# A buffer pool of their own for the gates' results, and three DMAs instead of eight for each piece of the SwiGLU weights' sums

## The chip, the cores and the metric

The kernel runs on one core of a Trainium2 chip. A core has TensorE (PE in the profile: matmuls; PEld is its loading of weights), VectorE (DVE), ScalarE (ACT), GpSimd (POOL) and SyncE (SP), which here issues all DMAs. TensorE writes to PSUM, of which this kernel uses eight banks of 128 x 512 float32; everything else lies in SBUF or in HBM. The metric is the device time of one execution in microseconds, smaller is better.

## The reference

The input x has 512 tokens of 1024 channels, all in float32. One decoder block is computed:

```
h = rmsnorm(x, norm1_g);  z = h @ w_in + b_in          # 1024 -> 6656
z_glu, z_rx, z_rg, z_ga, z_gb = split(z)               # 2048, 1280, 1280, 1024, 1024
u  = z_glu[:, :1024] * sigmoid(z_glu[:, 1024:])
u  = silu(layernorm(depthwise_conv31(u)));             y_a = u @ conv_w_out + conv_b_out
xb = depthwise_conv4(z_rx)
r, i = sigmoid(xb @ wa + ba), sigmoid(xb @ wx + bx)    # block-diagonal, 16 blocks of 80
a  = exp(-8 r softplus(-lambda));  b = sqrt(1 - a^2) * (i * xb)
hb = scan over tokens: hb[t] = a[t] hb[t-1] + b[t]
y_b = (hb * gelu(z_rg)) @ lru_w_out
x  = x + (sigmoid(z_ga) * y_a + sigmoid(z_gb) * y_b) @ w_mix_out
h  = rmsnorm(x, norm2_g)
x  = x + (silu(h @ ffn_w1) * (h @ ffn_w3)) @ ffn_w2    # SwiGLU, 2816 wide
out = rmsnorm(x, norm_f_g)
```

## The kernel before

**Number format.** A float32 operand is split into a high part and a low remainder (`split_to`, L115: ScalarE casts the high part, L117; VectorE or POOL subtracts, L113), and each product is three matmuls: high x high, high x low, low x high (`mm3`, L428).

**Weights.** All weight tiles stand in one list, in the order of their use (`wchunk`, L132). `emit_chunk` (L135) loads the next into one of four raw buffers (`raws`), splits it into one of five buffers (`hls`), and `weights` keeps the list four tiles ahead of the matmuls (`AHEAD`).

**First part, channels on partitions.** The list `ORDER` (L201) interleaves the tiles of z, 128 channels by 512 tokens each: `u` (GLU, two tiles of z), `rx` (input of the recurrence, `xb`, its split parts and the pieces `ext` of neighbouring blocks that DMAs copy, L697), `g` (gates), `r` (recurrence), `rg`, `gb` and `ga`. VectorE's 31 taps of the long convolution (`cv`, L596) are run a few at a time beside all of them.

A gate, `gates(j)` (L702), makes two PSUM banks of 4 or 6 matmuls each (L717). ScalarE takes Tanh of the first into the buffer `th` (L722) and of the second in place (L723), then Exp into the buffer `ea` (L726) and another Tanh in place (L727); VectorE follows with L728 to L731, where L731 is the last to read the first bank. `th` and `ea` last until the recurrence of the same number, `recur(j)` (L736), which takes a bank `mu` of its own for the square root (L739), multiplies (L740) and scans (L741). In `ORDER` no more than three gates stand between their `g` and their `r`.

**Buffers.** `tiles(tag, bufs)` (L91) makes a pool of buffers of 128 x 512. `longt` has 65 (`SLOTS`) and holds nearly everything that lasts: the normalized input, `u`, `xb`, `th`, `ea`, the sigmoids, the products and later the operands of the last matmuls. `shortt` has 5. PSUM has six banks for matmuls (`bank`) and two for convolution and the like (`bank2`).

**Later parts.** `yb` (L784) and `ya` (L895) are the two output projections. `w_mix_out`, part of SwiGLU's first weights (k = 2 to 5, `SEVEN`) and `ffn_w2` are multiplied as 2 x 2 blocks in seven products instead of eight, for which four sums t1 to t4 of the weights' blocks are needed. `Sevenfold.pair` (L821) makes the operands of k (`s1p`, `e`, and their parts), `run` (L842) the products. For w_mix_out and ffn_w2 the sums are made by `make_sums` (L276) on VectorE, in raw buffers. For SwiGLU's first weights `make_f_sums` (L314) makes them during the first part: there are 16 pieces; of each, four DMAs load four blocks of 128 x 256 into a buffer of the pool `wsums` (two buffers, L332), POOL makes four sums in place (L337 to L340), and four DMAs store them (L345) into DRAM tiles, one for each sum and k. A DMA of `f_chunk` (L307) reads a whole sum back as a weight tile during SwiGLU.

**Who sets the order.** The kernel is not written as queues. A planner takes the program and lays out each engine's queue before it runs: what is ready by its own estimates goes first, in the order of the code among what is ready. An instruction that writes a new buffer needs a free one of its pool. At run time each engine takes its queue in order, and semaphores hold back an instruction whose operands or buffers are not ready. `issue_after` puts an instruction behind a named one of the same engine; the weight sums' loads and stores stand behind the newest load of a weight tile (`newest["load"]`), and POOL's sums behind its newest subtraction. Some parts (the start, the end of the mix) are laid out by hand.

Of the kernel before, what the change touches and what calls it, by code (L numbers as in the profile page):

```python
# [8 lines left out]
F32 = mybir.dt.float32  # L9
# [4 lines left out]
P = 128  # L14
T = 512
# [13 lines left out]
NF = DF // P  # L29


SLOTS, SHORT = 65, 5
RAW = 4
HL = 5
AHEAD = 4
# [8 lines left out]
SEVEN = (2, 3, 4, 5)  # L44
# [36 lines left out]
def tile_block(ctx, tc, a, out):  # L81
    nc = tc.nc
# [8 lines left out]
    def tiles(tag, bufs):  # L91
        p_ = pool(tag, bufs)
        return lambda name, dtype=F32: p_.tile([P, T], dtype, tag=tag, name=name)

    longt, shortt = tiles("long", SLOTS), tiles("short", SHORT)

    def pairt(name, dtype=F32R):

# [13 lines left out]
    def sub(eng, o, x, y):  # L112
        return eng.tensor_tensor(out=o, in0=x, in1=y, op=ALU.subtract)  # L113
# [18 lines left out]
    def wchunk(key, src, kt, cols, where="hl", lo=pool_e, after=None):  # L132
        chunks.append((key, src, kt, cols, where, lo, after))
# [89 lines left out]
    dram = ctx.enter_context(tc.tile_pool(name="dram", bufs=1, space=bass.MemoryType.DRAM))  # L223
# [68 lines left out]
    w1 = a["ffn_w1"][0].rearrange("(k p) n -> p k n", p=P)  # L292
    w3 = a["ffn_w3"][0].rearrange("(k p) n -> p k n", p=P)


    KF = NF // 2
    f_sums = {(n, k): dram.tile([P, 1024], F32, tag=f"f{n}_{k}", name=f"f{n}_{k}") for k in SEVEN for n in ("t1", "t2", "t3", "t4")}

    def f_quarter(n, k, w_, c0, c1):

        c, j = 4 * (int(n[1]) - 1), k + KF * (int(n[2]) - 1)
        return w_[:, c + c0 : c + c1, j * P : (j + 1) * P]

    def f_chunk(n, k):
        def load(raw_t):
            if n[0] == "t":
                nc.sync.dma_start(raw_t, f_sums[n, k][:, :])  # L307
            else:
                for i, w_ in enumerate((w1, w3)):
                    nc.sync.dma_start(raw_t[:, i * T : (i + 1) * T].rearrange("p (k n) -> p k n", k=4), f_quarter(n, k, w_, 0, 4))  # L310

        wchunk(f"f{n}_{k}", load, 8, P, lo=vec)

    def make_f_sums():  # L314

        todo = [(k, i, c) for k in SEVEN for i in range(2) for c in (0, 2)]
        sums_due, stores_due = [], []
        n = 0  # L320
        while todo or sums_due or stores_due:
            if stores_due and emitted[0] >= stores_due[0][0]:
                stores_due.pop(0)[1]()
            if sums_due and n >= sums_due[0][0]:
                sums_due.pop(0)[1]()
            if todo and n >= SUMS_AT and (n - SUMS_AT) % SUMS_STEP == 0:
                k, i, c = todo.pop(0)
                raw = wsums.tile([P, 1024], F32, tag="wsum", name=f"fws{k}_{i}_{c}")
                q = [raw[:, 256 * m : 256 * m + 256] for m in range(4)]
                with tc.issue_after(newest["load"]):  # L330
                    for m, v in zip(("b11", "b12", "b21", "b22"), q):
                        nc.sync.dma_start(v.rearrange("p (k n) -> p k n", k=2), f_quarter(m, k, (w1, w3)[i], c, c + 2))  # L332

                def sums(q=q, k=k, at=T * i + P * c):
                    q11, q12, q21, q22 = q
                    with tc.issue_after(newest["sub"]):
                        sub(pool_e, q22, q22, q12)  # L337
                        sub(pool_e, q12, q12, q11)
                        pool_e.tensor_tensor(out=q11, in0=q22, in1=q11, op=ALU.add)
                        sub(pool_e, q21, q21, q11)  # L340

                    def stores():
                        with tc.issue_after(newest["load"]):
                            for m, v in (("t1", q12), ("t2", q11), ("t3", q22), ("t4", q21)):
                                nc.sync.dma_start(f_sums[m, k][:, at : at + 256], v)  # L345
# [24 lines left out]
    at, col, parts = 0, {}, []  # L370
    for name, n in ROWS:
# [4 lines left out]
        while done < n:  # L376
            m = min(n - done, P - row_at(at + done)[1])
# [161 lines left out]
    ab, e, s, s2, po, c4 = (sm[:, i, :] for i in range(6))  # L539
# [162 lines left out]
    def gates(j):  # L702
        hv, lv = (gate_view(v[:, 0, :]) for v in weights(f"gate{j}"))
        j5 = j % 5
        banks = []
        for g in range(2):
            ps = bank(f"g{j}_{g}")
            (wh, oh), (wl, ol) = ((v[:, g, 0, :], v[:, g, 1, :]) for v in (hv, lv))
            xh, xl = xbp[j]
            mms = [(wh, xh), (wh, xl), (wl, xh)]  # L710
            if j5 % 2:
                eh, el = ext[j]
                mms += [(l[:MANY], r[:MANY]) for l, r in ((oh, eh), (oh, el), (ol, eh))]
            else:
                mms.append((oh[: 3 * FEW], ext[j][0][: 3 * FEW]))
            for k, (l, r) in enumerate(mms):
                pe.matmul(ps, l, r, start=k == 0, stop=k == len(mms) - 1)  # L717
            banks.append(ps)

        r_, i_ = banks  # L720
        th = longt(f"th{j}")
        act.activation(th, r_, AF.Tanh, scale=0.5, bias=bh[:, 0, j : j + 1])  # L722
        act.activation(i_, i_, AF.Tanh, scale=0.5, bias=bh[:, 1, j : j + 1])  # L723
# [4 lines left out]
        vec.scalar_tensor_tensor(out=r_, in0=A, scalar=1.0, in1=r_, op0=ALU.add, op1=ALU.mult)  # L728
        vec.scalar_tensor_tensor(out=xb[j], in0=i_, scalar=1.0, in1=xb[j], op0=ALU.add, op1=ALU.mult)
        vec.tensor_scalar(out=A, in0=r_, scalar1=1.0, scalar2=None, op0=ALU.add)  # L730
        vec.scalar_tensor_tensor(out=th, in0=A, scalar=1.0, in1=r_, op0=ALU.add, op1=ALU.mult)  # L731
        rec[j] = A, th

    rec = {}

    def recur(j):  # L736
        A, m2 = rec.pop(j)
        mu = bank(f"mu{j}")
# [67 lines left out]
    class Sevenfold:  # L806
# [14 lines left out]
        def pair(self, k, ua, va):  # L821

            n = self.name
            u_ = split(f"{n}us{k}", ua, vec)
            s1 = shortt(f"{n}s1{k}")[:, LO]
            add(s1, va[:, LO], va[:, HI])
            sp = longt(f"{n}s1p{k}", F32R)
            split_to(sp[:, LO], sp[:, HI], s1, vec)
            e = longt(f"{n}e{k}")
            sub(vec, e[:, HI], ua[:, LO], va[:, LO])  # L830
            sub(vec, va[:, LO], s1, ua[:, LO])
            sub(vec, e[:, LO], ua[:, HI], va[:, LO])
            self.ops.append((u_, sp, e, va))
# [58 lines left out]
    for n, j in enumerate(mixq.order()):  # L892
# [3 lines left out]
        o = sga[j]  # L896
# [262 lines left out]
```

## Time and profile before

| | us |
|---|---|
| median of 3 runs (lowest, highest) | 814.06 (813.77, 814.31) |
| the profiled execution | 816.61 |
| its span, first to last instruction | 814.8 |
| TensorE busy | 801.8 (98%) |
| VectorE busy | 648.0 (80%) |
| ScalarE busy | 445.2 (55%) |
| POOL busy | 210.2 (26%) |
| moved by DMA | 153.47 MB, 188 GB/s in the mean |

All rows but the first are of one profiled execution. Its own time is 2.55 above the median of the runs, so a sum of its durations is compared with 816.61. Times in the text count from its first instruction. A row of a timeline gives start, duration, engine, line, operation, what is written and read, and in brackets the idle time of the engine before it and what ended that. A row of waits gives who waited for whom, the total in us, the number and the longest. Rows for the 40 slices of the span give the busy share in tenths; `PEclk` is TensorE's granted clock. Durations of matmuls overlap, since they are pipelined: their cost is the distance from start to start. Names of tiles stand without the buffers' numbers.

### The profile page before, as it was taken

The page shows a single profiled execution, that of the slowest core. Times are in us where ns is not written, and L with a number is a line of the kernel's source. Part 1 is how long each engine was busy: PE and PEld are TensorE (multiplying, and loading weights), DVE is VectorE, ACT ScalarE, POOL GpSimd, SP SyncE. Part 2 cuts the span into 40 slices and gives each one's busy share as a digit, 9 for nine tenths or more (in the row PEclk, how much of TensorE's full clock was granted, in tenths as well). Part 3 has the DMA queues.
Part 4 walks back from the last instruction along what each step waited for, and adds up shares of the span by engine and source line. Part 5 has one row for each costly group of instructions (what it writes and reads, how often), then busy time and mean ns, then how long its engine had stood idle before and what let it go on. Part 6 is the DMA issues. An engine that isn't in the chain of part 4 may idle for free.

```text
span 814.8 us, 11572 instructions
## 1 busy us (share of the span) xinstructions
PE 801.8 (98%) x4038; PEld 683.9 (84%) x4038; DVE 648.0 (80%) x1010; ACT 445.2 (55%) x627; POOL 210.2 (26%) x156
## 2 busy tenths in 40 slices
PE   8999999999999999999999999999999999999996
PEld 7988888887788888888888898999988888888885
DVE  4699899999999987787868869797866665688556
ACT  7546688777668855554336454374632233476443
POOL 3565778758665740000000042000000000000000
PEclk9999999999999999999999999999999999999998
DMA  7746466567565532358737525788778788576552
GB/s 209 192 123 163 131 186 204 169 192 194 163 190 156 167 88 65 101 174 256 234 106 245 156 92 177 243 251 262 227 237 264 251 286 283 185 261 210 173 167 104
DMA packets 183309, 153.47 MB, mean 188 GB/s; under 512 B 13799, under 2 KB 151443, under 8 KB 183251
## 3 DMA queue, kind: packets, MB, share of 16 engines
q1 hardware_dynamic: 183251, 152.73, 61.1%
q8 instruction: 32, 0.52, 0.3%
q14 instruction: 26, 0.21, 0.1%
HBM read 123.46 MB, written 26.21 MB: 184 GB/s over the span
## 4 chain that ended last, share of the span: by engine, by line
PE 92%; DVE 3%; DMA 1%; issue 1%; SPq 1%; POOL 0%; ACT 0%; POOLq 0%
PE z L437 31%; PE f L437 19%; PE or L840 13%; PE fr L1016 10%; PE yb L437 7%; PE ya L437 5%; PE mxr L840 5%; PE g L717 2%; DMA raw_in<-in_w_in_dram 1%; DVE cv L596 1%; SPq L393 1%; PE th L477 0%; DVE xb8l L113 0%; SPq L386 0%; POOL hl_in L113 0%
## 5 line engine op out<-in xcount | busy, mean ns | idle before, releaser
L596 DVE SCALAR_TENSOR_TENSOR cv<-u,par,cv 128x511 f32<-128x511 f32 (+17 forms) x240 | 162.8, 730 | 1.1 <-ACT cv L593 0.9
L113 POOL TENSOR_TENSOR hl_in<-raw_in,hl_in 128x1024 fp32r<-128x1024 f32 x52 | 125.4, 2415 | 92.7 <-ACT hl_in L117 90.2
L117 ACT CAST hl_in<-raw_in 128x1024 fp32r<-128x1024 f32 x52 | 54.2, 1043 | 10.2 <-PE z L437 6.6
L117 ACT CAST hl_f<-raw_f 128x1024 fp32r<-128x1024 f32 x28 | 29.3, 1051 | 51.4 <-DMA raw_f<-in_ffn_w_dram 37.7
L113 DVE TENSOR_TENSOR hl_f<-raw_f,hl_f 128x1024 fp32r<-128x1024 f32 x28 | 36.3, 1308 | 16.4 <-ACT hl_f L117 16.4
L990 POOL TENSOR_TENSOR hf<-h20h,h20l 128x512 f32<-128x512 f32 x1 | 1.3, 1287 | 172.4 <-DVE h20l L481 172.4
L117 ACT CAST hl_ob<-raw_ob 128x1024 fp32r<-128x1024 f32 (+1 forms) x23 | 23.4, 1016 | 38.9 <-PE or L840 18.6
L437 PE MATMUL z<-h10h,hl_in 128*128 128x512 f32 (+1 forms) x112 | 42.9, 385 | 1.5 <-DVE xb L741 1.2
L113 DVE TENSOR_TENSOR hl_ob<-raw_ob,hl_ob 128x1024 fp32r<-128x1024 f32 (+1 forms) x23 | 27.1, 1177 | 20.3 <-ACT hl_ob L117 20.2
L437 PE MATMUL z<-h11h,hl_in 128*128 128x512 f32 (+1 forms) x112 | 42.2, 378 | 0.0
L437 PE MATMUL z<-h12h,hl_in 128*128 128x512 f32 (+1 forms) x112 | 41.9, 376 | 0.0
L437 PE MATMUL z<-h15h,hl_in 128*128 128x512 f32 (+1 forms) x112 | 41.7, 374 | 0.0
L437 PE MATMUL z<-h14h,hl_in 128*128 128x512 f32 (+1 forms) x112 | 41.7, 374 | 0.0
L437 PE MATMUL z<-h13h,hl_in 128*128 128x512 f32 (+1 forms) x112 | 41.7, 374 | 0.0
L437 PE MATMUL z<-h16h,hl_in 128*128 128x512 f32 (+1 forms) x112 | 41.7, 374 | 0.0
L437 PE MATMUL z<-h17h,hl_in 128*128 128x512 f32 (+1 forms) x112 | 41.7, 374 | 0.0
L113 POOL TENSOR_TENSOR fws<-fws 128x256 f32<-128x256 f32 x48 | 36.3, 756 | 2.4
L113 DVE TENSOR_TENSOR ows<-ows,ows 128x512 f32<-128x512 f32 x22 | 15.2, 690 | 19.8 <-DMA ows<-in_ffn_w_dram 19.7
L113 DVE TENSOR_TENSOR hl_ot<-raw_ot,hl_ot 128x1024 fp32r<-128x1024 f32 (+1 forms) x17 | 20.1, 1191 | 11.8 <-ACT hl_ot L117 11.4
L117 ACT CAST hl_ot<-raw_ot 128x1024 fp32r<-128x1024 f32 (+1 forms) x17 | 17.5, 1028 | 17.2 <-PE or L840 15.5
L437 PEld LDWEIGHTS z<-h10h,hl_in 128*128 128x128 f32 x112 | 21.4, 191 | 6.3 <-ACT g L723 1.6
L437 PEld LDWEIGHTS z<-h11h,hl_in 128*128 128x128 f32 x112 | 21.4, 191 | 3.9
(905 smaller groups left out, 2582.3 us busy)
## 6 DMA issues: line engine op xcount, KB each, us to landing
raw_in<-in_w_in_dram SPq DMA_DIRECT2D x52, 512.0 KB
raw_f<-in_ffn_w_dram SPq DMA_DIRECT2D x28, 512.0 KB
ows<-in_ffn_w_dram SPq DMA_DIRECT2D x22, 512.0 KB
ot<-ows SPq DMA_DIRECT2D x44, 256.0 KB
raw_ob<-in_ffn_w_dram SPq DMA_DIRECT2D x33, 256.0 KB
raw_ot<-ot SPq DMA_DIRECT2D x33, 256.0 KB
fws<-in_ffn_w_dram SPq DMA_DIRECT2D x64, 128.0 KB
ft<-fws SPq DMA_DIRECT2D x64, 128.0 KB
```

The source lines that it names most:

```text
L113: return eng.tensor_tensor(out=o, in0=x, in1=y, op=ALU.subtract)
L117: copy(h, full)
L393: nc.sync.dma_start(xt[t][h], x_nat[:, t, h * T : (h + 1) * T])
L437: pe.matmul(ps, l, r, start=i == 0, stop=i == n - 1)
L596: vec.scalar_tensor_tensor(out=acc[c][:, s:], in0=u[c][:, : T - s], scalar=dw(c, s), in1=acc[c][:, s:], op0=ALU.mult, op1=ALU.add)
L717: pe.matmul(ps, l, r, start=k == 0, stop=k == len(mms) - 1)
L840: pe.matmul(banks[i], l_[:, ts], r_, start=start and n == 0, stop=stop and n == 2, skip_group_check=again)
L990: pool_e.tensor_tensor(out=v, in0=h2p[c][0].bitcast(F32), in1=h2p[c][1].bitcast(F32), op=ALU.add)
L1016: pe.matmul(ps[:, HALVES[i]], lw[:, 4 * i + c, :], rx_, start=not (again or i or c or m), stop=bool(i and c == 3 and m == 2), skip_group_c ...
```

## The change

First, the pool of 65 becomes one of 59, and a new pool of six buffers, `gatet`, takes `th` and `ea` of the gates. In the last stage the operands `oe0` to `oe5` of the last product's first six k take buffers of the new pool too. The number of buffers together stays 65.

Second, the four sums of SwiGLU's first weights of one k lie in one DRAM tile of 128 x 4 x 1024 in the order in which they stand in the SBUF buffer (t2, t1, t4, t3). So a piece is stored by one DMA instead of four. It is loaded by two DMAs instead of four, each of them two neighbouring blocks of 128 x 256. The sums themselves, and when they are asked for, are the same. The read back takes the same amount from the new tile, whose rows of 4 KB for one sum lie 16 KB apart.

```diff
-SLOTS, SHORT = 65, 5
+SLOTS, SHORT, GATES = 59, 5, 6
...
-    longt, shortt = tiles("long", SLOTS), tiles("short", SHORT)
+    longt, shortt, gatet = tiles("long", SLOTS), tiles("short", SHORT), tiles("gate", GATES)
...
-    f_sums = {(n, k): dram.tile([P, 1024], F32, tag=f"f{n}_{k}", name=f"f{n}_{k}") for k in SEVEN for n in ("t1", "t2", "t3", "t4")}
+    F_SUMS = ("t2", "t1", "t4", "t3")
+    f_sums = {k: dram.tile([P, 4, 1024], F32, tag=f"fs{k}", name=f"fs{k}") for k in SEVEN}
...
-                nc.sync.dma_start(raw_t, f_sums[n, k][:, :])
+                nc.sync.dma_start(raw_t, f_sums[k][:, F_SUMS.index(n), :])
...
+                four = (w1, w3)[i].rearrange("p (h k) (e n) -> p h k e n", h=2, e=2)
                 with tc.issue_after(newest["load"]):
-                    for m, v in zip(("b11", "b12", "b21", "b22"), q):
-                        nc.sync.dma_start(v.rearrange("p (k n) -> p k n", k=2), f_quarter(m, k, (w1, w3)[i], c, c + 2))
+                    for h in range(2):
+                        nc.sync.dma_start(
+                            raw[:, h * T : h * T + T].rearrange("p (e k n) -> p e k n", e=2, k=2),
+                            four[:, h, c : c + 2, :, k * P : (k + 1) * P].rearrange("p k e n -> p e k n"),
+                        )
...
-                            for m, v in (("t1", q12), ("t2", q11), ("t3", q22), ("t4", q21)):
-                                nc.sync.dma_start(f_sums[m, k][:, at : at + 256], v)
+                            nc.sync.dma_start(f_sums[k][:, :, at : at + 256], raw.rearrange("p (m n) -> p m n", m=4))
...
-        th = longt(f"th{j}")
+        th = gatet(f"th{j}")
...
-        A = longt(f"ea{j}")
+        A = gatet(f"ea{j}")
...
-            e = longt(f"{n}e{k}")
+            e = (gatet if n == "o" and k < GATES else longt)(f"{n}e{k}")
```

More of the change, by code (lines that the diff above doesn't have):

```diff
@@ L329, in make_f_sums, with sums @@
                 q = [raw[:, 256 * m : 256 * m + 256] for m in range(4)]
+                four = (w1, w3)[i].rearrange("p (h k) (e n) -> p h k e n", h=2, e=2)
                 with tc.issue_after(newest["load"]):
-                    for m, v in zip(("b11", "b12", "b21", "b22"), q):
-                        nc.sync.dma_start(v.rearrange("p (k n) -> p k n", k=2), f_quarter(m, k, (w1, w3)[i], c, c + 2))
-                def sums(q=q, k=k, at=T * i + P * c):
+                    for h in range(2):
[3 more added lines that the diff above has]
+                        )
+                def sums(raw=raw, q=q, k=k, at=T * i + P * c):
                     q11, q12, q21, q22 = q
```

## The prediction

> **What bounds the kernel now.** I read, in this order: the page's busy times and slices, the waits of TensorE, TensorE's timeline where those waits lie, then the timelines of ScalarE and VectorE just ahead of them, and last the issues of the weight sums' DMAs on SP.
>
> ```profile
> PE 801.8 (98%) x4038; PEld 683.9 (84%) x4038; DVE 648.0 (80%) x1010; ACT 445.2 (55%) x627; POOL 210.2 (26%) x156
> PE   8999999999999999999999999999999999999996
> DVE  4699899999999987787868869797866665688556
> PEclk9999999999999999999999999999999999999998
> ```
> ```profile
> PE z L437 <- DVE xb L741: 1.2, 1, 1.2
> ...
> PE g L717 <- DVE th L731: 0.6, 1, 0.6
> ```
>
> TensorE is the bound: from 26 to 805 us its slices are full. One 128x512 matmul starts 0.227 us after the one before it (202.56 after 202.33 below). So whatever does not take a gap out of TensorE's row gives nothing, and there are few gaps to take. After the start-up only two waits exceed half a microsecond, both for VectorE, and both lie in one place:
>
> ```profile
> 202.01 0.48 PE L717 MATMUL g<-xb7h,hl_gate 128*128 128x512 f32 x1
> 202.33 0.39 PE L717 MATMUL g<-xb7l,hl_gate 128*128 128x512 f32 x1
> 202.56 0.40 PE L717 MATMUL g<-xb7h,hl_gate 128*128 128x512 f32 x1
> ...
> 203.82 0.50 PE L717 MATMUL g<-xb7h,hl_gate 128*128 128x512 f32 x1 [0.63 <-DVE th L731]
> ...
> 206.24 0.77 PE L437 MATMUL z<-h10h,hl_in 128*128 128x512 f32 x1 [1.22 <-DVE xb L741]
> 206.80 0.63 PE L437 MATMUL z<-h10l,hl_in 128*128 128x512 f32 x1
> ...
> 209.72 0.39 PE L437 MATMUL z<-h12h,hl_in 128*128 128x512 f32 x1
> ```
>
> From 202.01 to 206.24 lie 8 matmuls (8 x 0.227 = 1.82), so 4.23 - 1.82 = 2.41 us were stood. The next 8, from 206.24 to 209.72, took 3.48 us at half the granted clock instead of 1.82: 1.66 more. The place costs 4.07 us. TensorE waits there for PSUM banks: gate 7's second bank was gate 6's first (read last by L731), the next `z` bank was that of recurrence 4 (read last by the scan, L741). Why these were late:
>
> ```profile
> 185.88 0.66 ACT L723 ACTIVATE g<-g,bh 128x512 f32<-128x512 f32 x1 [0.88 <-PE g L717]
> ...
> 189.78 0.62 ACT L117 CAST xb8h<-xb 128x512 fp32r<-128x512 f32 x1 [2.27 <-DVE xb L674]
> ...
> 192.31 0.68 ACT L722 ACTIVATE th<-g,bh 128x512 f32<-128x512 f32 x1
> ```
> ```profile
> 197.44 3.31 DVE L596 SCALAR_TENSOR_TENSOR cv<-u,par,cv 128x501 f32<-128x501 f32 x5
> 200.66 0.68 DVE L728 SCALAR_TENSOR_TENSOR g<-ea,g 128x512 f32<-128x512 f32 x1
> ...
> 203.10 0.67 DVE L731 SCALAR_TENSOR_TENSOR th<-ea,g 128x512 f32<-128x512 f32 x1
> ```
>
> Gate 6 writes two Tanh. The code has `th` (L722) first, and its bank was complete by 184.5. Yet L723 ran at 185.88, ScalarE then sat idle 2.27 us, and `th` came at 192.31, right behind `xb8h`. The difference: L722 writes a new buffer of the pool of 65, L723 writes in place. Laying the code's list of those buffers on their first writes in the trace, I find them in the code's order but for some microseconds throughout: `th6` is asked for behind `xb8`, `xb8h`, `xb8l`, and came behind them. Gates 1, 2 and 4 show the same inversion (second Tanh at 87.7, 109.2, 138.2; first at 91.3, 114.5, 139.7).
>
> **The change part by part.**
>
> *Gates' own pool.* `th6` no longer stands behind the `xb8` buffers. The six gate buffers last belonged to gate 3 and were free at 161.6, so `th6` can run beside the second Tanh at about 186, 6.3 us earlier. The chain behind it (Exp 0.82, Tanh 0.76, L728 to L731 3.1) moves with it, by up to 6.3 us: the bank wanted at 202.9 is then free at about 197, and of the 2.3 us by which recurrence 4's bank was late for 203.8, the three gate operations taken out of VectorE's last stretch give 2.0 (3 x 0.68), and the square roots at 200.4, moved ahead on a freer ScalarE, the rest. Bounds: nothing (the wait stands) to -4.07 (both waits and the half clock go). I take -4.07, since both banks' lateness is the chain's. What is late next: nothing within the next microseconds; margins below.
>
> The half-clock stretch follows the stand: the granted clock is 1.00 up to 206.2, half to 209.6, and 1.00 again. The Trainium skill (TensorE: Matmul & The Clock Gate, "What's actually happening") puts the throttle after an idle window of about 3.4 us; here 2.4 us of stand in two pieces were enough, so trace and page differ. By the page alone, removing the stand would not remove the 1.66 us, and the sum would be -2.41.
>
> The pool's own waits: a gate now waits for the gate three before it. The trace never holds more than six such buffers (144 to 156 and 196 to 206 us), so six suffice; the tightest is `ea7` at 207.03, 0.94 us behind the end of the scan that frees `ea4`. Behind `ea7` on ScalarE stand weight casts, and no weight tile of `z` is split less than 7.2 us before its first matmul: cost 0, with that cover gone at most the lateness of the scan.
>
> *59 buffers for the rest.* Without gates' buffers and `oe0` to `oe5` the trace holds 60 four times: over by one for 0.19 us at 310.8, 0.19 at 316.1, 0.42 at 322.1 and 5.76 at 370.2 to 376.0 (`mxt41l`, until `yb7` frees `y0`). The first three delay a sigmoid or a cast while the PSUM banks near there have over 3 us to spare: 0. The fourth holds one of four raw buffers, so the mix weights' load at 371.07 and, behind it in SP's queue, that of conv_w_out at 375.14 issue up to 5.8 us later; that tile is split 11.0 us before its matmul: 0, and even the whole 5.8 is under 11.0. From 688 to 703 all 65 are held before and 59 + 6 after: no difference. From 720 to 742 the rest holds up to 61: the splits `oeb`, `ovb` wait about one step of k (18 x 0.227 = 4.1 us). Those of k = 7 to 10 are used from 776 on (747.5 + 7 x 4.1): 0, upper bound in the rivals. `oe0` to `oe5` find the gate pool empty since 272.
>
> *Three DMAs a piece.*
>
> ```profile
> L332 SPq DMA_DIRECT2D fws<-in_ffn_w_dram x64: 383/468/697, 34.9 to 255.1; - x64
> L345 SPq DMA_DIRECT2D ft<-fws x64: 383/480/1232, 66.1 to 275.5; - x64
> ```
> ```profile
> SPq L332 <- DMA ft<-fws: 18.5, 16, 3.4
> ```
>
> Before: 64 x 0.468 + 64 x 0.480 = 60.7 us of SP. After: 32 loads of 256 KB in 512 B pieces (nearest row: `raw_fb`, same size and piece, 0.499) = 16.0, and 16 stores of 512 KB (nearest: `raw_in`, 512 KB, 0.385; `ft`, 1 KB pieces, 0.480) = 6.2 to 7.7. SP gains 37 to 39 us. Bytes and pieces stay: 512 B in, 1 KB out, 4 KB back. A load still waits for the store two pieces before (18.5 us in 16 waits, at most 3.4); the store starts as one, up to 3 x 0.48 = 1.4 us of issue sooner, but lands whole, so that wait grows by at most 1.4 x 14 = 20 us, less than is freed. Queued behind are the loads of `z` weights and gates, with the 7.2 us above. TensorE's list has no wait for a weight's DMA, so this gives 0; as bounds I take -0.3 (the wait for hl_in, all that TensorE lists for `z` weights) and +1.4 (one store's issue uncovered once). POOL's 64 operations are the same. The read back has the same 4 KB pieces, only further apart; the nearest tile (`hl_ft4_2`) has 1.7 us to spare: 0.
>
> *Sum.* -4.07 + 0. The profiled execution took 816.61 (span 814.8): 812.5. The median shown, 814.06, is 2.55 below that execution; the same step from it gives 810.0.
>
> **The rivals.**
>
> *The stall stays or moves (814.1).* All engines' queues are laid out anew in advance, and VectorE stays as full (281.1 busy of the 300 us from 30 to 330) on the same six banks. Margins elsewhere are thin: the banks of `z23` (161.1), `z33` (261.5) and `z4` (111.2) were free 0.67, 0.73 and 0.89 us before use. Against: these too hang on gates or recurrences, which come earlier. One like the present gives 814.1; two give 818.1.
>
> *Split waits in the last stage (slower).* Place: 720 to 748, k = 7 to 10, where 59 buffers are up to two short. Price: if ScalarE stands one step (4.1) at a split ahead of a weight cast, a tile with 2.9 (747.5) or 4.05 us (727.1) to spare is up to 1.2 us late; with a half clock, 2.9. Four times: 810.0 + 11.6 = 821.6. It decides from two on (815.8). For: ScalarE already follows TensorE by 0.06 to 2 us there. Against: the casts stand earlier in the code.
>
> *The half clock stays (811.6).* If the slow stretch came by itself, only 2.41 goes: 811.6. Against: it begins at the 206.2 at which TensorE resumes.
>
> **How the numbers follow.** Forecast 0.55, its own range 809.0 to 811.8 (a remaining wait of up to 1.8). Stall stays or moves 0.20; two stalls 0.10; last stage 0.10; half clock 0.05. About 0.2% (1.6 us) is what a measurement of this kernel can tell from no change. Faster (below 812.4): 0.55 + 0.05 less the edges, 0.59; same: 0.20; slower: 0.21. The range 809.0 to 818.5 holds all but most of the last-stage case, the upper half of two stalls and a little below 809.
>
> **What would show it.** Right: in every gate L722 directly beside L723; no wait of TensorE for L731 or L741; granted clock 1.00 from 30 to 800; 32 loads and 16 stores on the sums' lines; SP's wait there under 39 us. Wrong: a new wait of TensorE for VectorE between 60 and 330 with a half-clock slice behind it; one for ScalarE's casts between 720 and 760; or L722 still behind casts of `xb`.

## The result, and the profile after

The changed kernel takes 819.36 us (median; 818.94 to 820.82), the kernel before, beside it, 814.18 (813.32 to 816.03). The ratio is 1.0064 (95% interval 1.0053 to 1.0074): slower by 5.2 us, where 4.1 us less was forecast. The profiled execution took 819.27 (span 817.4) against 816.61. The line numbers of the changed kernel are larger by up to 5: L717 of before is L722 now, L722 and L723 are L727 and L728, L731 is L736.

The engines' totals, from the page of the changed kernel:

```profile
PE 801.2 (98%) x4038; PEld 684.6 (84%) x4038; DVE 646.3 (79%) x1010; ACT 443.0 (54%) x625; POOL 211.2 (26%) x156
```

They say nothing; each is within 3 us of before. The waits of TensorE in the changed kernel do (who waits for whom, total, number, longest):

```profile
PE g L722 <- DMA ext<-xb6h: 4.4, 1, 4.4
...
PE fr L1021 <- ACT c L1033: 0.7, 1, 0.7
```

The two waits of gate 7, for L731 and the scan, are gone, as forecast. A wait at gate 5 has come, not for VectorE but for a DMA: the copies of `xb6`'s rows into `ext5`. TensorE's timeline there:

```profile
159.27 0.39 PE L722 MATMUL g<-xb5h,hl_gate 128*128 128x512 f32 x1
164.02 0.47 PE L722 MATMUL g<-ext,hl_gate 96*128 96x512 f32 x1 [4.36 <-DMA ext<-xb6h]
...
165.28 0.63 PE L722 MATMUL g<-ext,hl_gate 96*128 96x512 f32 x1
...
168.21 0.39 PE L442 MATMUL z<-h12h,hl_in 128*128 128x512 f32 x1
```

From 159.27 to 164.02 are 4.75 us for one step of 0.227: 4.52 stood. The 11 steps from 164.02 to 168.21 took 4.19 instead of 2.50, most of them at half the granted clock: 1.69 more. The place costs 6.2 us. A wait of 0.7 in SwiGLU (L1021, at 543.4) costs 0.8. Against that stand the 4.07 that went at gate 7: +2.9, and the two profiled executions differ by 2.66.

At gate 7 the mechanism of the forecast worked. VectorE's last read of gate 6's first bank:

```profile
198.55 0.68 DVE L736 SCALAR_TENSOR_TENSOR th<-ea,g 128x512 f32<-128x512 f32 x1
```

It starts 4.5 us earlier than the 203.10 of before, though TensorE came to gate 7 5.7 us later (207.7 against 202.0); the bank was free in time for either. ScalarE now takes gate 6's first Tanh at 190.58 and the second at 193.30, in the code's order; in all ten gates the first now comes ahead of the second, where in four of before it came behind.

The DMAs of the weights' sums in the changed kernel (minimum, median and maximum ns, start of first and last), and SP's wait for their stores:

```profile
L335 SPq DMA_DIRECT2D fws<-in_ffn_w_dram x32: 602/643/740, 34.5 to 255.7; - x32
L350 SPq DMA_DIRECT2D fs<-fws x16: 571/596/1768, 66.0 to 275.5; - x16
```
```profile
SPq L335 <- DMA fs<-fws: 41.3, 11, 6.3
```

SP spends 32 x 0.643 + 16 x 0.596 = 30.1 us on issuing instead of 60.7, and waits 41.3 instead of 18.5, once 6.3 us.

Where the lateness of the copies comes from is seen by going back along the queues. Around 140 us the changed kernel has, on ScalarE, GpSimd and SP:

```profile
142.37 0.62 ACT L118 CAST xb5h<-xb 128x512 fp32r<-128x512 f32 x1 [6.31 <-DVE xb L679]
142.89 1.04 ACT L118 CAST hl_in<-raw_in 128x1024 fp32r<-128x1024 f32 x1
...
148.30 0.60 ACT L118 CAST hl_gate<-raw_gate 128x512 fp32r<-128x512 f32 x1
```
```profile
144.01 3.01 POOL L114 TENSOR_TENSOR hl_in<-raw_in,hl_in 128x1024 fp32r<-128x1024 f32 x1 [6.80 <-ACT hl_in L118]
...
154.23 0.52 POOL L184 MEMSET raw_gate<- 128x512 f32 x1
```
```profile
152.56 1.35 SPq L335 DMA_DIRECT2D fws<-in_ffn_w_dram  x2
154.01 0.58 SPq L145 DMA_DIRECT2D raw_in<-in_w_in_dram  x1
154.78 2.85 SPq L189 DMA_DIRECT2D raw_gate<-in_lru_wa_dram  x5
157.68 2.57 SPq L189 DMA_DIRECT2D raw_gate<-in_lru_wx_dram  x4
160.37 0.57 SPq L702 DMA_DIRECT2D ext<-xb6h  x1
```

The same steps in the kernel before:

```profile
136.68 0.62 ACT L117 CAST xb5h<-xb 128x512 fp32r<-128x512 f32 x1
...
139.22 0.62 ACT L117 CAST hl_gate<-raw_gate 128x512 fp32r<-128x512 f32 x1
```
```profile
147.97 0.54 POOL L183 MEMSET raw_gate<- 128x512 f32 x1
```
```profile
154.55 0.54 SPq L697 DMA_DIRECT2D ext<-xb6h  x1
```

`xb5h` is 5.7 us late and the first copy 5.8. `xb5` itself is late on VectorE: its three operations start at 138.9 instead of 133.2, behind 96 taps of the long convolution where it stood behind 90 (a tap takes 0.65 us, so the six are 3.9). The rest comes from two waits of VectorE for ScalarE near 101 us, 0.62 ahead of a `u` and 1.35 ahead of a tap, which the kernel before does not have. The experiments ask which part of the change does this, and which of these links carries it.

### The profile page after: what moved, and what is told of

Same layout as the page of the kernel before. It is cut to its first block, busy times and chain, and to the rows that moved or that the text cites. A ratio compares the mean times of both kernels' runs of the same rounds, so it can differ in the third digit from the quotient of the medians.

```text
span 817.4 us, 11473 instructions
## 1 busy us (share of the span) xinstructions
PE 801.2 (98%) x4038; PEld 684.6 (84%) x4038; DVE 646.3 (79%) x1010; ACT 443.0 (54%) x625; POOL 211.2 (26%) x156
## 2 busy tenths in 40 slices
DMA packets 182029, 153.46 MB, mean 188 GB/s; under 512 B 12519, under 2 KB 150163, under 8 KB 181971
## 4 chain that ended last, share of the span: by engine, by line
PE 80%; DVE 13%; DMA 3%; ACT 2%; POOL 1%; issue 1%; SPq 0%; POOLq 0%; ACTq 0%; DVEq 0%
PE z L442 26%; PE f L442 16%; PE or L845 13%; PE yb L442 7%; PE fr L1021 6%; PE ya L442 5%; DVE cv L601 5%; PE mxr L845 5%; PE g L722 1%; DVE xb L679 1%; PE tx L482 1%; DVE hl_fb L114 1%; DMA raw_ft<-fs 1%; POOL hl_in L114 1%; DMA raw_fb<-in_ffn_w_dram 1%
## 5 line engine op out<-in xcount | busy, mean ns | idle before, releaser
L601 DVE SCALAR_TENSOR_TENSOR cv<-u,par,cv 128x511 f32<-128x511 f32 (+16 forms) x240 | 162.2, 728 | 2.3 <-ACT cv L598 2.2
L442 PE MATMUL z<-h16h,hl_in 128*128 128x512 f32 (+1 forms) x112 | 41.7, 374 | 0.0
L442 PE MATMUL z<-h17h,hl_in 128*128 128x512 f32 (+1 forms) x112 | 41.7, 374 | 0.0
L114 DVE TENSOR_TENSOR ows<-ows,ows 128x512 f32<-128x512 f32 x22 | 15.2, 689 | 20.8 <-DMA ows<-in_ffn_w_dram 20.6
L679 DVE SCALAR_TENSOR_TENSOR xb<-z,par,xb 128x511 f32<-128x511 f32 (+2 forms) x30 | 22.2, 741 | 4.2 <-ACT xb L677 4.0
```

Source lines behind the costliest of these rows:

```text
L442: pe.matmul(ps, l, r, start=i == 0, stop=i == n - 1)
L601: vec.scalar_tensor_tensor(out=acc[c][:, s:], in0=u[c][:, : T - s], scalar=dw(c, s), in1=acc[c][:, s:], op0=ALU.mult, op1=ALU.add)
L679: vec.scalar_tensor_tensor(out=o[:, s:], in0=ps[:, : T - s], scalar=lw(s), in1=o[:, s:], op0=ALU.mult, op1=ALU.add)
```

## The experiments

Every kernel ran beside the kernel before on the same chip; its median was 814.68, 815.17, 814.68 and 814.80 in the four groups. "Stood" is the distance between two neighbouring starts of TensorE less 0.227. The start-up of the profiled executions differs: its last matmul comes between 26.3 and 28.2 us, and all times behind it move with that.

### One part of the change alone

Theory 1: the single store lands late, the next load into its buffer waits, and the copies behind it come late. Rival 1: the gates' pool alone lays the queues out anew, and that makes them late. The gates' pool alone:

```diff
-SLOTS, SHORT = 65, 5
+SLOTS, SHORT, GATES = 59, 5, 6
...
-        th = longt(f"th{j}")
+        th = gatet(f"th{j}")
...
-        A = longt(f"ea{j}")
+        A = gatet(f"ea{j}")
...
-            e = longt(f"{n}e{k}")
+            e = (gatet if n == "o" and k < GATES else longt)(f"{n}e{k}")
```

> The gates' pool (59 + 6 buffers) alone; loads and stores of the sums as before. Theory 1 (the single store lands late, the next load waits for it in SP's queue, and the DMAs of ext behind it come late for gate 5): no single store, so no stand at gate 5, and the stand at gate 7 is gone too: 810 to 812. Rival 1 (the gates' pool lays the queues out so that xb6 and ext come late, whatever the stores do): the stand at gate 5 stays, 817 to 820. Rival 2 (only both together do it): 810 to 812 here and about 814 for the DMAs alone.

The three DMAs alone (pool of 65; the lines that declare the tensors are those of the change), and each half of them:

```diff
...
-                    for m, v in zip(("b11", "b12", "b21", "b22"), q):
-                        nc.sync.dma_start(v.rearrange("p (k n) -> p k n", k=2), f_quarter(m, k, (w1, w3)[i], c, c + 2))
+                    for h in range(2):
+                        nc.sync.dma_start(
+                            raw[:, h * T : h * T + T].rearrange("p (e k n) -> p e k n", e=2, k=2),
+                            four[:, h, c : c + 2, :, k * P : (k + 1) * P].rearrange("p k e n -> p e k n"),
+                        )
...
-                            for m, v in (("t1", q12), ("t2", q11), ("t3", q22), ("t4", q21)):
-                                nc.sync.dma_start(f_sums[m, k][:, at : at + 256], v)
+                            nc.sync.dma_start(f_sums[k][:, :, at : at + 256], raw.rearrange("p (m n) -> p m n", m=4))
```

> Three DMAs a piece alone, pool of 65 as before. Theory 1: SP's wait of the sums' loads for the stores is about 40 us as with the whole change, against 18.5 before, and TensorE stands for ext or for a gate: 816 to 820. Rival 1: as before, 813 to 815, with the stand at gate 7. Rival 2: 813 to 815, SP's wait long but met by nobody.

The second of these two hunks without the first:

```diff
...
-                            for m, v in (("t1", q12), ("t2", q11), ("t3", q22), ("t4", q21)):
-                                nc.sync.dma_start(f_sums[m, k][:, at : at + 256], v)
+                            nc.sync.dma_start(f_sums[k][:, :, at : at + 256], raw.rearrange("p (m n) -> p m n", m=4))
```

> One store a piece instead of four, four loads as before, pool of 65. Theory 1: SP's wait for stores is over 30 us; the time is that of the DMAs alone, within 1 us. If the wait is under 25 us, the loads of two blocks each are the slow part.

The first without the second:

```diff
-                    for m, v in zip(("b11", "b12", "b21", "b22"), q):
...
+                    for h in range(2):
...
```

> Two loads a piece instead of four, four stores as before, pool of 65. Theory 1: SP's wait for stores stays near 18.5 us, 813 to 815. Rival (the loads of 4-dimensional form are what is slow, 0.64 us of issue each against 0.47): SP's wait grows here.

| kernel | us (lowest, highest) | ratio to before (95%) | TensorE stood |
|---|---|---|---|
| gates' pool alone | 819.11 (817.65, 819.27) | 1.0052 (1.0037, 1.0067) | 4.5 at gate 5, then half clock |
| three DMAs alone | 814.78 (813.57, 817.47) | 1.0002 (0.9992, 1.0012) | 0.5 and 0.3 at gates 6 and 7, 1.4 behind gate 7 |
| one store alone | 814.89 (813.85, 816.24) | 1.0002 (0.9991, 1.0014) | gate 7 as before |
| two loads alone | 815.38 (814.06, 817.11) | 1.0005 (0.9994, 1.0017) | gate 7 as before |

Waits of TensorE with the gates' pool alone:

```profile
PE g L717 <- DMA ext<-xb6h: 4.4, 1, 4.4
```

This is the wait of the changed kernel, with all eight DMAs a piece. Theory 1 falls: the gates' pool alone makes the kernel slower, by 4.4 us, and the three DMAs alone, though SP's wait for stores grew from 18.5 to 30.2 us with them, make no difference that can be measured. With one store alone that wait was 27.5 us, short of the 30 expected, with two loads alone 19.7.

### What in the gates' pool: taps ahead of u4

With the gates' pool the planner has gate 2's operations on VectorE earlier, and seventeen taps that the code writes behind `u4` run ahead of it (nine before): `u4` starts at 130.67 instead of 124.39. Theory 2: VectorE, filled up with taps, makes `xb5` and `xb6` late. First, the gates' pool with each tap planned behind the newest `u`:

```diff
-        vec.scalar_tensor_tensor(out=uj, in0=pv, scalar=b_in(GLU + j), in1=sg, op0=ALU.add, op1=ALU.mult)
+        newest["u"] = vec.scalar_tensor_tensor(out=uj, in0=pv, scalar=b_in(GLU + j), in1=sg, op0=ALU.add, op1=ALU.mult).ins
...
-                    vec.scalar_tensor_tensor(out=acc[c][:, s:], in0=u[c][:, : T - s], scalar=dw(c, s), in1=acc[c][:, s:], op0=ALU.mult, op1=ALU.add)
+                    with tc.issue_after(newest["u"]):
+                        vec.scalar_tensor_tensor(out=acc[c][:, s:], in0=u[c][:, : T - s], scalar=dw(c, s), in1=acc[c][:, s:], op0=ALU.mult, op1=ALU.add)
```

> The gates' own pool, and every tap of the depthwise convolution is planned behind the newest u that the code has written (a constraint on the planner alone). Theory 2 (with the gates' pool the planner places seventeen later-written taps of 0.65 us ahead of u4 on VectorE, where it placed nine before; xb5 and xb6 follow late, and gate 5 stands): u4 starts near 122 instead of 130.67, xb6h near 150 to 152 instead of 154.6, the copies of xb6's rows are issued near 155 to 157 instead of 160.0, gate 5 stands under 1 us instead of 4.77, no half clock there; without gate 7's stall as well the time is 811 to 814. Rival 2 (the gates' six buffers themselves, by their order of reuse, hold the work up): u4 moves, but the stand of over 3 us stays at gate 5 or comes back at another gate; 817 to 820.

Measured: 812.99 us (811.47 to 814.06), ratio 0.9977 (0.9967 to 0.9987). `u4` starts at 126.23 (later than expected), `xb5` at 134.5 behind 80 taps, the copies are issued at 155.23, and TensorE stands at neither gate; 0.65 us are left at 256.5. So the six buffers hold nothing up by themselves, and the order of VectorE matters.

The reverse, on the kernel before: seventeen taps brought forward and `u4` planned behind the last of them (taps brought forward are left out later, by the counter `ahead`).

```diff
...
+        if j == 4:
+            run_beside(17)
+            ahead[0] = 17
+        if j == 4:
+            with tc.issue_after(newest["tap"]):
+                vec.scalar_tensor_tensor(out=uj, in0=pv, scalar=b_in(GLU + j), in1=sg, op0=ALU.add, op1=ALU.mult)
...
```

> The kernel before with its one pool of 65 and its eight DMAs a piece; seventeen taps that are written behind u4 are written ahead of it, and u4 is planned behind the last of them, so that seventeen stand ahead of it in VectorE's queue where nine did. Theory 2: u4 starts 5 us later (129.6), xb6 is 2 to 4 us later, gate 5 stands 1.5 to 4.5 us, and the time rises to 816 to 819, without any change of the pools. Rival 2 (only the pool of its own makes it): gate 5 does not stand, 813.5 to 815.5. The taps that were brought forward are missing later, so xb5 and xb6 may catch up; a stand under 1.5 us would leave the question half open.

Measured: 812.62 (812.26 to 813.17), ratio 0.9968 (0.9956 to 0.9979): faster, a miss for theory 2. `u4` did start at 128.58, behind 89 taps as with the gates' pool, but the planner took other taps out behind it: `xb5` starts at 134.3, `xb6h` is made at 150.15, the copies are issued at 153.46. Taps ahead of `u4` don't matter by themselves. Gate 7's stall shrank to 0.64 on the way.

The copies on another queue, to part SP's share from VectorE's:

```diff
-                    nc.sync.dma_start(ext[key][d][at0 : at0 + nr, :].bitcast(F32), src[k])
+                    nc.scalar.dma_start(ext[key][d][at0 : at0 + nr, :].bitcast(F32), src[k])
```

> The gates' own pool; the copies of the overlap rows (xb's rows into ext) are issued by ScalarE's queue instead of SP's. In the kernel with the gates' pool xb6h was ready at 155.2 and xb6l at 157.0, but the copies were issued by SP at 160.0 to 161.2, behind seven loads of raw_gate6. Theory 2 in full (VectorE late by about 4 us and SP's queue by a further 3): gate 5 stands 0.8 to 1.8 us instead of 4.77, time 814 to 816. If VectorE's lateness alone makes the stand: 4 us or more stay, 818 to 820. If SP's queue alone makes it: under 0.3 us, 811 to 814.

Measured: 838.37 (837.11 to 839.61), ratio 1.0286 (1.0269 to 1.0303). All three expectations miss, since the run does not tell what it was made for: a copy that waits now holds up ScalarE. Its timeline:

```profile
174.43 0.59 ACT L117 CAST y1h<-z 128x512 fp32r<-128x512 f32 x1 [7.75 <-DMA ext<-xb6h]
```

ScalarE did nothing for 7.75 us before that cast, and gate 5 waited 8.2 us. It says nothing on SP's share.

### The three DMAs once more, with the taps in order

> The whole change (gates' pool and three DMAs a piece) with the same constraint on the taps. Theory 2, with the DMAs worth nothing: as the gates' pool with that constraint alone, 811 to 814, no stand over 1 us at gates 5 and 7. If the three DMAs cost something beside the gates' pool: 1 to 3 us above that kernel.

The whole change with each tap behind the newest `u`, as above: 817.08 (815.29 to 819.16), ratio 1.0026 (1.0012 to 1.0040), 4.1 us more than with eight DMAs a piece. VectorE's queue is the same in both. Waits of TensorE:

```profile
PE g L723 <- DMA ext6h<-xb7h: 1.3, 1, 1.3
...
PE g L723 <- DMA ext<-xb6h: 0.9, 1, 0.9
```

So the three DMAs are not free once VectorE is punctual. SP's timeline, first with eight DMAs, then with three:

```profile
143.04 2.29 SPq L345 DMA_DIRECT2D ft<-fws  x4
149.89 1.92 SPq L332 DMA_DIRECT2D fws<-in_ffn_w_dram  x4
```
```profile
144.65 0.71 SPq L350 DMA_DIRECT2D fs<-fws  x1
151.38 1.36 SPq L335 DMA_DIRECT2D fws<-in_ffn_w_dram  x2
```

The load into the buffer is issued 4.6 us after the last of four stores (149.89 - 145.33), and 6.0 us after the single one (151.38 - 145.36). Counted from the start of the first store's issue it is 6.9 and 6.7 us: the buffer comes free hardly sooner with one store, and the issue that SP saves comes back as waiting. The Trainium skill (DMA: Bandwidth & Descriptors, "Anatomy of one DMA", written for DMAs that GpSimd issues) says that a DMA's semaphore is raised only when its last byte is confirmed to have landed; the two rows fit that, since the load starts microseconds after the last issue has ended. Behind that load stand gate 6's loads and then the copies of `xb6` (157.27 instead of 155.23), and the copies of `xb7` (181.30 instead of 178.85; 0.7 us of either difference is start-up, since `xb5` starts at 135.21 instead of 134.48). Which half of it is to blame, and whether it is the wait, three runs asked. Two loads and four stores (hunk and taps as above):

> Gates' pool and taps behind the newest u, with two loads and four stores a piece. VectorE's queue is the same as with eight DMAs (812.99) and as with three (817.08). If the single store costs the difference of 4.1 us (its landing is waited for by the next load into the same buffer, and behind that load stand the copies of xb6 and xb7): 811.5 to 814.0, gates 5 and 6 stand under 0.5 us each. If the larger loads cost it: 816 to 818.

Four loads and one store:

> Gates' pool and taps behind the newest u, with four loads and one store a piece. If the single store costs the 4.1 us: 815.5 to 818.5, with stands of 0.5 to 2 us at gates 5 and 6 as with three DMAs. If the larger loads cost it: 811.5 to 814.0.

Three buffers for the sums, so that a load waits for an older store (paid for by two of the five buffers of `shortt`):

```diff
-SLOTS, SHORT, GATES = 59, 5, 6
+SLOTS, SHORT, GATES = 59, 3, 6
...
-    wsums = pool("wsums", 2)
+    wsums = pool("wsums", 3)
```

> The whole change with taps behind the newest u, and with three buffers for the sums instead of two (paid for by two of the five short buffers), so that a load does not wait for the store issued last but for the one before. If the wait for the store's landing is what costs 4.1 us: 811.5 to 814.5, SP's total wait for a store under 15 us instead of about 40. If the transfers themselves or their issue cost it: 816 to 818. Three short buffers instead of five may cost something of their own in later stages; a stand there would show by its place.

| gates' pool, taps behind the newest u | us (lowest, highest) | ratio (95%) | SP waits for stores | first copy of xb6, of xb7 | the same from xb5's start | TensorE stood at gates 5, 6, L1021 |
|---|---|---|---|---|---|---|
| 4 loads, 4 stores | 812.99 (811.47, 814.06) | 0.9977 (0.9967, 0.9987) | 25.7 | 155.23, 178.85 | 20.8, 44.4 | 0, 0, 0 |
| 2 loads, 4 stores | 817.52 (814.72, 819.19) | 1.0026 (1.0010, 1.0041) | 30.1 | 156.09, 181.42 | 22.3, 47.7 | 1.3, 3.2, 1.5 |
| 4 loads, 1 store | 816.95 (815.73, 818.65) | 1.0029 (1.0017, 1.0040) | 37.1 | 156.96, 181.60 | 21.3, 45.9 | 0, 2.5, 0.4 |
| 2 loads, 1 store | 817.08 (815.29, 819.16) | 1.0026 (1.0012, 1.0040) | 36.4 | 157.27, 181.30 | 22.1, 46.1 | 1.1, 2.0, 0.9 |
| 2 loads, 1 store, 3 buffers | 813.92 (813.70, 815.40) | 0.9995 (0.9985, 1.0005) | 12.6 | 153.09, 176.15 | 18.7, 41.7 | 0, 0, 0.2 |

Either half costs what both cost, so neither "the store alone" nor "the loads alone" holds. What the three dear kernels share is the place of the copies: `xb7`'s are issued 1.5 to 3.3 us later, counted from `xb5`'s start, and gate 6, which reads them, stands in all three. Part of that is the wait (the next load is issued at 150.89 with two loads, 151.50 with one store, 149.89 with eight DMAs), part is the order: with eight DMAs two of gate 7's loads still stand behind the copies of `xb7`, in the three others all of them stand ahead, with a load of `z` weights. With three buffers even more loads stand ahead of them and the copies still go 2.7 us earlier than with eight DMAs, and TensorE stands at neither gate: the wait is what makes the order hurt. By the ratios some 1.5 us against eight DMAs remain. The profiled execution has 1.1 of them at its very end, 8.50 us from the last matmul's start to the end where all the other kernels take 7.42 or 7.43. VectorE waits there for an output to leave one of the three buffers that `shortt` still has:

```profile
807.83 0.69 DVE L1088 TENSOR_TENSOR of<-x2b,gfh 128x512 f32<-128x512 f32 x1 [1.77 <-DMA out_dram<-of]
```

So that part is the price of the two buffers, and not of the three DMAs. The wait at L1021 was 0.8 us in the changed kernel and 0.2 to 1.5 in the four kernels with the gates' pool, ordered taps and merged DMAs, and absent with eight DMAs or the old pool; its cause was not followed.

### Which link makes gate 5 stand

On the kernel before, `xb6` alone made late: the first of its operations planned behind the 107th tap (before: the 101st).

```diff
...
         for s in range(1, KL):
-            vec.scalar_tensor_tensor(out=o[:, s:], in0=ps[:, : T - s], scalar=lw(s), in1=o[:, s:], op0=ALU.mult, op1=ALU.add)
+            with tc.issue_after(tap(107) if j == 6 else first):
+                vec.scalar_tensor_tensor(out=o[:, s:], in0=ps[:, : T - s], scalar=lw(s), in1=o[:, s:], op0=ALU.mult, op1=ALU.add)
```

> The kernel before, with its pool of 65 and its DMAs; only the first of xb6's three operations on VectorE is planned behind the 107th tap, where it stood behind the 101st (in the kernel with the gates' pool alone, behind the 106th). VectorE's queue is the same up to there. Theory 2, as the runs so far leave it (what counts is not how many taps stand ahead of u4 but how many ahead of xb6: six more are 3.9 us): xb6's operations start near 151 instead of 147.3, its copies are issued 4 to 6 us later than 154.5, gate 5 stands 3 to 6 us and goes on at half clock, and the time is 816 to 820, with no change of any pool. If the gates' pool itself is needed for the stand: under 1 us at gate 5, 813.5 to 815.5.

Measured: 812.78 (811.98 to 814.07), ratio 0.9976 (0.9967 to 0.9986). A miss again: `xb6` starts at 150.5 and `xb6l` at 155.0, but gate 5 stands 0.55 us only, since SP had all of gate 6's loads behind it by 153.6 and issued the copies at 156.51. With the gates' pool alone `xb6l` started at 156.3, the copies went at 160.01, behind seven loads for gate 6 that had waited for GpSimd to clear `raw_gate6` (at 155.95; here at 146.76). This points to a chain over GpSimd. Theory 3: `xb5` late on VectorE makes `xb5h` late on ScalarE, and with it the casts `hl_in13` and `hl_gate5` queued behind; GpSimd follows these, clears `raw_gate6` late, and SP's loads and copies wait for that. It is an order that suits a punctual VectorE. Three runs on the kernel before. First `xb5` late, behind the 96th tap (the cut is against the run above):

```diff
-            with tc.issue_after(tap(107) if j == 6 else first):
+            with tc.issue_after(tap(96) if j == 5 else first):
```

> The kernel before, with its pool and its DMAs; the first of xb5's three operations on VectorE is planned behind the 96th tap, as in the kernel with the gates' pool alone, where it stood behind the 90th. The planner is free to answer that on the other queues, and puts the casts of hl_in13 and hl_gate5 ahead of xb5h on ScalarE. Theory 3 (what makes gate 5 stand is not VectorE's lateness by itself but what is queued behind it in an order that was planned for a punctual VectorE: ScalarE's cast xb5h, behind it the casts of hl_in13 and hl_gate5, behind these GpSimd's work and the clearing of raw_gate6, behind that SP's loads and the copies of xb6): with the casts ahead the chain is cut, gate 5 stands under 1 us, 812 to 814.5. Theory 2 (a late VectorE alone is enough, at xb5 where it was not at xb6): gate 5 stands 2 us or more, 815 to 819.

Then, added to that, the orders of the gates' pool put back on ScalarE and GpSimd:

```diff
+    behind = {"in13": "xb5h", "gate5": "g4"}
...
+            if key in behind:
+                with tc.issue_after(newest[behind[key]]):
+                    h, l = split_to(hl[:, 0, :n], hl[:, 1, :n], rv, lo)
...
+            if j == 6:
+                with tc.issue_after(newest["f3_1_0"]):
+                    pool_e.memset(raw[:, :512], 0.0)
```

> As the kernel with xb5 behind the 96th tap, with three orders of the kernel with the gates' pool put back: hl_in13's cast behind xb5h, hl_gate5's cast behind the last of gate 4's activations, and the clearing of raw_gate6 behind all four sums of the piece 3_1_0 on GpSimd. Pool of 65, eight DMAs. Theory 3: xb5h near 140.5, hl_in13 on GpSimd near 142, raw_gate6 cleared near 154.5 (147.97 before, 155.95 with the gates' pool), the copies of xb6 issued at 157 to 158.5, gate 5 stands 1.5 to 3.5 us; 814.5 to 817.5, and above the kernel of the other two by 2 us or more. If the gates' buffers themselves are needed: under 0.7 us at gate 5, 812 to 814.

And these orders with a punctual `xb5` (against the run before it):

```diff
-            with tc.issue_after(tap(96) if j == 5 else first):
+            with tc.issue_after(first):
```

> The three orders alone (hl_in13's cast behind xb5h, hl_gate5's behind gate 4's activations, raw_gate6's clearing behind the four sums), with xb5 behind the 90th tap as before. Theory 3: xb5h is punctual (near 136.5), so the chain runs some 4 us earlier than with xb5 late: raw_gate6 cleared near 151.5, the copies of xb6 issued near 155.5, gate 5 stands under 0.7 us, 812 to 814.5. If the order on ScalarE and GpSimd is enough without a late VectorE: 1.5 us or more at gate 5, 814.5 to 817.5.

| kernel before, with | us (lowest, highest) | ratio (95%) | xb5h | raw_gate6 cleared | first copy | gate 5 stood |
|---|---|---|---|---|---|---|
| xb5 late | 812.94 (811.98, 814.70) | 0.9981 (0.9971, 0.9992) | 139.38 | 147.48 | 154.08 | 0 |
| xb5 late, casts behind | 815.21 (813.75, 817.74) | 1.0005 (0.9995, 1.0016) | 140.09 | 155.63 | 158.60 | 2.3 |
| casts behind | 812.66 (812.04, 813.46) | 0.9974 (0.9965, 0.9984) | 136.44 | 150.76 | 154.82 | 0 |

The second of the three, its waits of TensorE and its rows on ScalarE and GpSimd:

```profile
PE g L739 <- DMA ext<-xb6h: 2.2, 1, 2.2
```
```profile
140.09 0.62 ACT L118 CAST xb5h<-xb 128x512 fp32r<-128x512 f32 x1 [2.08 <-DVE xb L695]
...
146.82 0.60 ACT L118 CAST hl_gate<-raw_gate 128x512 fp32r<-128x512 f32 x1
```
```profile
155.63 0.53 POOL L190 MEMSET raw_gate<- 128x512 f32 x1
```

Only the two together make gate 5 stand, with the old pools and eight DMAs, and the kernel's median is 2.3 and 2.5 us above the other two. The stands tell 1.5 and 1.7 of it, since the other two still stand 0.84 and 0.64 at gate 7 and this one does not; the five of its ten runs at a mean clock of 0.994 are its five slowest, so the rest may be half clock behind the stand. Theory 3 holds for the gates' pool with eight DMAs. The stand is smaller than the 4.5 us of the gates' pool: only five loads of gate 6 were planned ahead of the copies, not seven, the copies went at 158.60 and not at 160.01, and `xb5` was 3.8 us late and not 6.2 (counted from the start-up's last matmul).

In the changed kernel two things hold gate 6's loads back equally long: SP is through with the piece's load, which waited for the single store, and a weight's at 154.59, and the clearing ends at 154.75. GpSimd, with another order there, clears earlier than with eight DMAs, and nine loads follow instead of seven. By these times the link over GpSimd alone is worth no more than 0.2 us there, and both would have to go. What stays open is why the planner, by its own estimates, puts more taps ahead of `xb5` once the gates have a pool of their own; the traces show only the order that came out.

## Why the prediction was wrong

**What bounds the kernel.** Right: TensorE is the bound, only its gaps count, and the changed kernel's time is again told by them.

**Gates' own pool, at its place.** The stall at gate 7 went, through the earlier L731, as forecast. But its cause was told too narrowly. With `xb6` late alone, `th6` still comes behind `xb8h` (192.22, second Tanh at 185.26), and the stall is down to 0.9 all the same; in the five kernels on the old pool that only had an order nudged, it was 0 to 0.9, and four of them came out faster than before. The inversion was one way to a late VectorE, not the only one.

**Gates' own pool, its bounds.** This is the step that failed: "Bounds: nothing (the wait stands) to -4.07". A loss was left out, though the step itself says that the planner asks for buffers in the code's order. Taking gates out of that order lays out all queues anew. It put six more taps ahead of `xb5` (3.9 us of its lateness), and what followed on ScalarE, GpSimd and SP made gate 5 stand 4.5 us and run on at half clock: +6.2 beside the -4.07, so +2.1 in the profiled execution where -4.07 was forecast.

**The size of the gain.** The term of 1.66 us for the half clock was taken at full size from the profiled execution. Most runs seem to lack it. A run's mean granted clock counts every half-clock stretch, also one at start-up, which the profiled execution of before has too (8.2 to 11.7 us); a clock of 0.998 belongs in the traces to none ahead of the end, 0.995 or 0.996 to one. Of the 99 runs of the kernel before beside the experiments, 38 had 0.997 or 0.998 (median 814.57). Of the 75 at 0.995 or more (median 814.61) none took over 815.78; the 14 runs of 815.96 and more are all among the 24 below 0.995 (median 816.00), and the profiled one (816.61, 0.993) was like these. So the stretch is probably the larger part of the 2.55 us between it and the median, which the prediction carried without asking what it was. For the median little more than the 2.41 us of stand could be won: the kernels with eight DMAs a piece in which it went or fell below 0.9, without a new one of over 0.7, are at 812.6 to 813.0, 1.9 to 2.6 us below before, not 4. For the medians the sum is then about +6.2 + 0.8 - 2.4 = 4.6 of the 5.2 measured.

**59 buffers.** Cost 0, as forecast: no wait of TensorE between 310 and 376 us or in the last stage.

**Three DMAs.** Issue was mis-sized: 0.643 and 0.596 us each against 0.499 and 0.385 to 0.480, so SP gains 30.6 us, not 37 to 39. The wait grew by 22.8 us, over the bound of 20, and in the changed kernel it cost nothing that the runs can tell (1.0064 against 1.0052 with the gates' pool alone; the trace has 0.8 us at L1021), as forecast. But "0" held only because something as late was in the way: with VectorE punctual the same DMAs cost 4 us, outside the bounds of -0.3 to +1.4. Weights were taken to be queued behind the loads; the copies into `ext`, on the same queue, were left out, and they have no 7.2 us to spare: before's last copy for gate 5 is issued at 157.68, and TensorE reads `ext` from 159.98 on.

**Rivals.** "The stall stays or moves" was the one that came, and `z23` at 161.1 was named as a thin place; the stand came 2 us ahead of that, for a copy and not for a bank. Its price, "one like the present gives 814.1", was too small, and "gates or recurrences, which come earlier" was no reason against it, since another engine's lateness decided. The last stage and the half clock by itself did not come; the half clock does follow a stand, though not each one (below).

## What to carry to other kernels

Where a planner lays out queues ahead of time, taking a few buffers out of a pool is not a local edit: price it by what the new order can make late on every engine, and let the range reach as far as the largest stand that the thinnest margin allows. Follow a thin DMA's whole queue: the copies that TensorE needs at once stood behind loads that waited for a store, and behind loads that waited for another engine. Before a gap in one profiled execution is priced, look whether the other runs have it. Here most of the 2.4 us of stand could be had by naming the order of two casts and one memset (812.66 against 814.80), without any new pool; three other nudges of one order (812.62 to 812.94) did as much, so this is the luck of a layout and not the merit of one order.

## What the runs showed of the hardware

The half clock after a stand comes by chance when the stand is short. In the profiled executions it followed before's stand of 2.4 us in two pieces all three times (the kernel before, one store alone, two loads alone), and yet the times and mean clocks above suggest that most runs of before lack it. In single executions it did not follow 1.7 us in two pieces (three DMAs alone), 2.0 (gate 6, three DMAs with ordered taps), 2.3 (`xb5` late, casts behind) or 2.5 (four loads, one store); it followed 2.5 us (at 113 us with the copies on ScalarE's queue), 3.2 (two loads, four stores) and, in both executions that had it, 4.5. At gates 5 to 7 each such stretch lasts 3.413 us in the kernels whose copies SP issues, and in the profiled execution of before it begins 57 such lengths (194.56 us) after the previous one ended, in that of the changed kernel 44 (150.19). The Trainium skill (TensorE: Matmul & The Clock Gate, "What's actually happening") speaks of a free-running window of that length and of results that vary from run to run; the runs agree, and the prediction, which set the page aside for its idle window of 3.4 us, read one run as a rule.

One store of 512 KB instead of four of 128 KB moves SP's time from issuing to waiting. From the start of a piece's first store to the next load into its buffer the median of 14 pieces is 5.7 us with four stores (before) and 5.5 with one (the changed kernel); from the end of the last issue it is 3.5 and 4.8.
